# Moving the first load of a streaming row mean ahead of the program's opening barrier

## The chip, the cores and the metric

The kernel runs on one core of a Trainium2 chip (trn2). The metric is the device time of one execution in microseconds (us).

## The reference

```python
def setup_inputs():
    return {"x": np.random.randn(64, 256, 8192).astype(np.float32)}

def reference(x: np.ndarray) -> np.ndarray:
    return np.mean(x, axis=2)
```

The input is 64 x 256 x 8192 x 4 bytes = 536.87 MB, read once; the output is 64 KB. There is one addition per element read.

## The kernel before

The 16384 rows are cut into 64 blocks of 256 rows, two rows to each of 128 partitions (8.39 MB a block). SyncE issues all loads into three slots, VectorE sums each block with one reduce instruction, and ScalarE helps only near the end. The last block is loaded in shrinking pieces, so that little work is left when the last byte has landed.

```python
ROWS, SLOTS, LOAD_SEMS = 2, 3, 6
FETCH_BLOCK = 128
LAST_CHUNKS = (4096, 2048, 1024, 512, 256, 256)
# ...
    slots = [nc.alloc_sbuf_tensor(f"xt{i}", [P, R, S], F32) for i in range(SLOTS)]
    load_sem = [tc.alloc_semaphore(f"load{i}") for i in range(LOAD_SEMS)]
    # ...
    nc.vector.addr_align(FETCH_BLOCK, offset=0, max_nops=0)   # VectorE's stream is aligned
    # ... identity matrix on GpSimd, two small memsets on VectorE
    def load(dst, src, sem):
        ld = untracked(nc.sync.dma_start(out=dst, in_=src))
        # ... (kept out of the framework's own semaphores)
        ld.then_inc(sem, 16)
        return ld
    # ...
    for n in range(LB):                                       # LB = 63
        xt = slots[n % SLOTS]
        load(xt[:], x_v[n], load_sem[n % LOAD_SEMS])
        if n < LB - 1:
            loaded(n, dve_sum(res[:, :, n], xt[:]))           # waits for load n
        # ... last block, transposes and stores
```

The framework puts a head in front of this body: each engine loads its registers, GpSimd fills four small constant tiles (0.24 to 0.44 us in the trace of before), each engine executes a drain that reports to a barrier (the first at 0.00 us, the last, GpSimd's own, done at 0.49), and nobody enters the body before GpSimd has collected all reports and released them (at 0.61 us; the others go on at 0.66 to 0.67).

## Time and profile before

| What | Value | Where it is read |
|---|---|---|
| device time | 1248.35 us median of 3 (1248.23 to 1248.42) | times |
| span | 1246.8 us | page |
| bytes over span | 431 GB/s, 99.6% DMA share | page |
| VectorE busy | 87% | page |
| first load issued | 0.74 us | chain, timeline |
| first load bytes move | 1.77 us | trace of DMA packets |
| first sum starts | 23.15 us | timeline |

These lines are from the page of the kernel before: the span, busy tenths of VectorE and of the DMA engines in 40 slices, GB/s per slice, the chain of waits by engine, and the costliest group (busy us, mean ns of one, then idle us before it and what ended it).

```profile
span 1246.8 us, 224 instructions
...
DVE  2898988989889889898898988989889888898897
...
DMA  9999999999999999999999999999999999999998
GB/s 404 437 437 437 435 431 418 431 437 437 437 437 437 435 433 418 429 437 437 437 437 437 435 431 414 435 437 437 437 437 435 437 429 416 435 437 437 437 437 339
...
DMA 70%; DVE 29%; SPq 0%; issue 0%; DVEq 0%
...
L95 DVE TENSOR_REDUCE res<-xt 128x2 f32<-128x16384 f32 (+1 forms) x63 | 1076.4, 17086 | 154.0 <-DMA xt<-in_x_dram 154.0
```

The DMA line is full from the first slice to the last but one, 99.6% over the span. VectorE looks busy but waits for a load before every sum: 63 waits, 154.0 us in total. So the stream is the limit. It moves 431 GB/s over the span and 437 in 22 of the 40 slices, the most that any slice of this trace shows. Whether it can be made faster was not tested here; as long as it is not, what remains is the time before it starts and the time after it ends.

The head is easiest to see in the chain of waits (start us, length us, what). In these views DVE is VectorE; SPq, DVEq and PEq are the instruction queues of SyncE, VectorE and TensorE; "issue" is time in which an engine waited for nothing that the profile shows. This is the chain of the kernel before, its head and its end:

```profile
0.67 0.07 issue
0.74 22.39 DMA xt<-in_x_dram
23.12 0.02 issue
23.15 17.23 DVE res L95
...
1203.09 38.48 DMA xt<-in_x_dram
1241.58 0.02 issue
1241.60 0.69 DVE fin_in L95
...
1243.66 0.21 DVE fin_t L112
```

Nothing in the chain comes before 0.67 us: that is where the barrier releases SyncE. SyncE's own list of waits (engine and line, waited for: us in total, times, longest) names the wait (PEq, TensorE's queue, is the last engine to report to GpSimd, at 0.32 us; the trace has GpSimd let the engines go at 0.61 us), and the busy table by stretches (start:end and length in us, five engines, then clock, DMA share, GB/s) shows that no byte moves in the first 1.7 us:

```profile
SPq L176 <- PEq L176: 0.7, 1, 0.7
```

```profile
0.00:1.00 1.00, 0.00 (x0) 0.00 (x0) 0.00 (x0) 0.00 (x0) 0.41 (x5) 1.00 0.00 0
1.00:1.70 0.70, 0.00 (x0) 0.00 (x0) 0.13 (x2) 0.00 (x0) 0.29 (x1) 1.00 0.00 0
1.70:3.00 1.30, 0.00 (x0) 0.00 (x0) 0.00 (x0) 0.00 (x0) 0.00 (x0) 1.00 2.32 807
```

The GB/s of a short stretch is not a rate, because a packet of 65536 bytes is booked where it starts, and the first sixteen of this trace take 2.4 to 3.4 us (3.0 in the mean). Zero is zero, however.

### The profile page before, as it was taken

Reading aid. Unit: us, or ns where it says so; the run is one execution under the profiler, and the core shown is the slowest. Engines: PE = TensorE matmul, PEld = TensorE weight load, DVE = VectorE, ACT = ScalarE, POOL = GpSimd, SP = SyncE. Lnnn points to the kernel's source line nnn. Section 1 sums busy time; section 2 is a strip of 40 time slices with the busy share of each in tenths; the row PEclk is TensorE's granted clock in tenths of the full one; section 3 lists DMA queues with packets and bytes.
Section 4 is the critical chain, followed back from the end, with each engine's and each line's share of the span. In section 5 each row is a group of like instructions: output and inputs, shape, how many; then the busy total and the mean of one; then the engine's idle time right before and its main releaser. Section 6 shows DMA issues by size and latency. Waiting matters only on the chain.

```text
span 1246.8 us, 224 instructions
## 1 busy us (share of the span) xinstructions
PE 0.9 (0%) x2; PEld 0.4 (0%) x2; DVE 1087.3 (87%) x79; ACT 16.5 (1%) x13; POOL 0.7 (0%) x6
## 2 busy tenths in 40 slices
PE   0000000000000000000000000000000000000000
PEld 0000000000000000000000000000000000000000
DVE  2898988989889889898898988989889888898897
ACT  0000000000000000000000000000000000000004
POOL 0000000000000000000000000000000000000000
DMA  9999999999999999999999999999999999999998
GB/s 404 437 437 437 435 431 418 431 437 437 437 437 437 435 433 418 429 437 437 437 437 437 435 431 414 435 437 437 437 437 435 437 429 416 435 437 437 437 437 339
DMA packets 10169, 536.95 MB, mean 431 GB/s; under 512 B 1145, under 2 KB 1464, under 8 KB 1720
## 3 DMA queue, kind: packets, MB, share of 16 engines
q1 hardware_dynamic: 10168, 536.94, 99.6%
q14 instruction: 1, 0.01, 0.0%
HBM read 536.87 MB, written 0.07 MB: 431 GB/s over the span
## 4 chain that ended last, share of the span: by engine, by line
DMA 70%; DVE 29%; SPq 0%; issue 0%; DVEq 0%
DMA xt<-in_x_dram 70%; DVE res L95 29%; DVE fin_in L95 0%; SPq L85 0%; DVE fin_in L101 0%; DVE fin_t L112 0%; DVEq L101 0%
## 5 line engine op out<-in xcount | busy, mean ns | idle before, releaser
L95 DVE TENSOR_REDUCE res<-xt 128x2 f32<-128x16384 f32 (+1 forms) x63 | 1076.4, 17086 | 154.0 <-DMA xt<-in_x_dram 154.0
L98 ACT ACT_TABLE_LOAD x1 | 1.3, 1283 | 1182.5 <-DVE res L95 1182.5
L98 ACT ACTIVATE xt<-xt 128x8192 f32<-128x8192 f32 (+5 forms) x6 | 14.7, 2443 | 43.9 <-DMA xt<-in_x_dram 43.7
L95 DVE TENSOR_REDUCE fin_in<-xt 128x1 f32<-128x256 f32 (+3 forms) x5 | 4.9, 1003 | 0.3 <-DMA xt<-in_x_dram 0.2
L95 DVE TENSOR_REDUCE head<-xt 128x1 f32<-128x4096 f32 x1 | 4.4, 4420 | 0.2 <-DMA xt<-in_x_dram 0.2
L154 PE MATMUL ps<-ident,res 128*63 128x128 f32 x2 | 0.9, 458 | 1231.5 <-ACT xt L98 1230.4
L75 DVE MEMSET fin<- 128x32 f32 x2 | 0.1, 85 | 1.4 <-PEq L176 1.4
L98 ACT ACTIVATION_READ_ACCUMULATOR xt<-xt 128x1 f32 x6 | 1.1, 186 | 0.0
L155 DVE TENSOR_SCALAR bulk<-ps 63x128 f32<-63x128 f32 x2 | 0.6, 278 | 0.4 <-PE ps L154 0.4
L154 PEld LDWEIGHTS ps<-ident,res 128*63 128x63 f32 x2 | 0.4, 180 | 1231.8 <-issue 1230.4
L101 DVE TENSOR_SCALAR_CACHE_REDUCE fin_in<-fin_in 128x265 f32<-128x265 f32 x1 | 0.4, 431 | 0.2 <-DVE fin_in L95 0.2
L112 DVE STREAM_TRANSPOSE fin_t<-fin 128x32 f32<-128x32 f32 x2 | 0.4, 211 | 0.1
L63 POOL TENSOR_SCALAR_AFFINE_SELECT ident<-ident 128x128 f32<-128x128 f32 x1 | 0.3, 292 | 0.1
L101 DVE TENSOR_SCALAR_CACHE_REDUCE head<-head 128x2 f32<-128x2 f32 x1 | 0.2, 155 | 0.1
L62 POOL MEMSET ident<- 128x128 f32 x1 | 0.2, 204 | 0.3 <-POOLq L176 0.3
L176 POOL MEMSET const-bfloat16-1.0<- 128x1 bf16 x1 | 0.1, 101 | 0.0
L176 POOL MEMSET const-uint8-127<- 128x1 uint8 x1 | 0.1, 101 | 0.0
L176 POOL MEMSET const-float32-0.0<- 128x1 f32 x1 | 0.1, 98 | 0.2 <-issue 0.2
L176 POOL MEMSET const-float32-1.0<- 128x1 f32 x1 | 0.1, 98 | 0.0
L101 DVE DVE_READ_ACCUMULATOR head<-head 128x1 f32 x1 | 0.1, 83 | 0.0
L101 DVE DVE_READ_ACCUMULATOR fin_in<-fin_in 128x1 f32 x1 | 0.1, 83 | 0.0
## 6 DMA issues: line engine op xcount, KB each, us to landing
xt<-in_x_dram SPq DMA_DIRECT2D x1, 4096.0 KB, 31.1
xt<-in_x_dram SPq DMA_DIRECT2D x1, 2048.0 KB, 35.7
xt<-in_x_dram SPq DMA_DIRECT2D x1, 1024.0 KB, 37.7
xt<-in_x_dram SPq DMA_DIRECT2D x63, 40.8
xt<-in_x_dram SPq DMA_DIRECT2D x1, 512.0 KB, 38.5
xt<-in_x_dram SPq DMA_DIRECT2D x1, 256.0 KB, 38.7
xt<-in_x_dram SPq DMA_DIRECT2D x1, 128.0 KB, 38.5
fin_in<-in_x_dram SPq DMA_DIRECT2D x1, 128.0 KB, 38.4
```

The lines of the kernel that those rows point to most:

```text
L62: nc.gpsimd.memset(ident[:], 0.0)
L63: nc.gpsimd.affine_select(out=ident[:], in_=ident[:], compare_op=mybir.AluOpType.not_equal, fill=1.0, base=0, pattern=[[-1, P]], channel_m ...
L75: nc.vector.memset(fin[r][:], 0.0)
L95: return untracked(nc.vector.tensor_reduce(out=dst, in_=src, axis=X, op=ADD))
L98: return untracked(nc.scalar.activation(out=src, in_=src, func=COPY, accum_out=dst))
L101: return nc.vector.tensor_scalar(out=src, in0=src, scalar1=inv, scalar2=None, op0=mybir.AluOpType.mult, op1=ADD, accum_out=dst,)
L112: nc.vector.transpose(out=fin_t[r][:], in_=fin[r][:])
L154: nc.tensor.transpose(out=ps[:LB, :], in_=res[:, r, :], identity=ident[:])
L155: nc.vector.tensor_scalar_mul(out=bulk[:LB, :, r], in0=ps[:LB, :], scalar1=inv)
L176: nc = _bacc.Bacc("TRN2", target_bir_lowering=False, num_devices=1)
```

## The change

The first load needs nothing that the barrier guards: its slot has not been touched and its semaphore is its own. The change takes this one instruction out of the body and puts it into the head, in front of SyncE's barrier drain. No instruction is added or removed.

```diff
     for n in range(LB):
         xt = slots[n % SLOTS]
-        load(xt[:], x_v[n], load_sem[n % LOAD_SEMS])
+        ld = load(xt[:], x_v[n], load_sem[n % LOAD_SEMS])
+        if n == 0:
+            first = ld
# ... at the end of the kernel:
+    ctx.close()
+    tc.close()
+    tc.compile()
+    head_bb, body_bb = nc.main_func.blocks[:2]
+    assert first.ins in body_bb.instructions
+    body_bb.instructions.remove(first.ins)
+    at = next(
+        i
+        for i, ins in enumerate(head_bb.instructions)
+        if ins.engine == first.ins.engine and isinstance(ins, mybir.InstDrain)
+    )
+    head_bb.instructions.insert(at, first.ins)
```

## The prediction

> **What bounds the kernel.** The stream from HBM. The page reports 431 GB/s over the span, a DMA share of 99.6%, and 9 or more tenths in all 40 slices but the last. VectorE is busy 87%, but in the list of waits its sums wait for loads 63 times, 154.0 us in total. In the chain of waits, loads take 70% and sums 29%; the sums are there because a load needs a free one of three slots. Each sum ends about 2.1 us before the next load lands. A load takes 40.8 us from issue to landing, about two load pitches of 19.35, so it queues behind others and the queue never runs dry. Where the stream starts sets where it ends; the last landing in the chain (1241.58 us) leads into a tail of 5.2 us to 1246.8.
>
> **The head, before.** SyncE's barrier record comes first (time 0); the other engines reach the barrier at 0.12 to 0.32 us, GpSimd's drain ends at 0.49, and SyncE is released at 0.66 (SyncE's list of waits: 0.7 us). The first load is issued at 0.74, its issue takes 0.42, and the first packet moves at 1.77, 1.03 us after the issue began. Loads two and three are issued at 1.23 and 1.67.
>
> **What the change does.** By the order of instructions only SyncE's stream differs: the first load stands before the barrier's drain. Nothing is added or removed. The load needs nothing that the barrier guards: its slot is untouched and its semaphore its own.
>
> - Off the critical path: the 0.74 us between SyncE's first record and the first load. I expect the issue at 0 to 0.05 us, first packets at 1.0 to 1.1, and every later landing 0.7 earlier.
> - Moved onto the barrier: one issue slot, 0.49 us (738 to 1226 ns). SyncE then arrives at about 0.5 us, about when GpSimd's drain ends, so the release slips by at most 0.1 us. This is off the critical path: the second load is issued before 0.9 us, while the first takes some 21 us to move.
> - The drain now stands behind a load: [...] I expect no wait for the landing. No run shows this yet.
>
> **Predicted time.** Stream and tail shift as one: 1248.35 - 0.70 = 1247.65 us, 0.06% faster; several times the spread of the three runs (0.2 us), far inside 2%. Range 1247.2 to 1248.3. Chances: faster by over 2% 0.002, within 2% 0.994, slower by over 2% 0.004.
>
> **What would show it.** First load issued near 0, first packets near 1.05; the first sum at about 22.4 instead of 23.15; the release near 0.7; all sums ahead of before by a constant 0.7; an unchanged tail of 5.2 us; span near 1246.1; GB/s barely changed.
>
> **What would make it wrong.** (1) The drain waits for the landing: the barrier is released near 22 us, the second load is late, the stream idles about 2 us, and the time is near 1250. (2) The issue ahead of the barrier costs more than 0.42 us, or its packets come later than 1.03 us after it. (3) Launch, not SyncE's first record, starts what is timed: if SyncE's first instruction comes later, the gain shrinks. (4) Another phase of the stream changes its rate: slices differ between 414 and 437 GB/s, and 0.1% of rate outweighs the gain.

The 2 us of idling under (1) is an estimate; the run with the forced wait below measured 2.0.

## The result and the profile after

| | before | changed |
|---|---|---|
| device time, median (range, runs) | 1248.43 us (1248.23 to 1248.86, 6) | 1247.71 us (1247.58 to 1247.82, 6) |
| span of the profiled run | 1246.8 us | 1246.0 us |
| first load issued | 0.74 us | 0.00 us |
| first load bytes move | 1.77 us | 1.04 us |
| barrier releases SyncE | 0.655 us | 0.740 us |
| second load issued | 1.23 us | 0.83 us |
| first sum starts | 23.15 us | 22.46 us |

The ratio is 0.9994 with a 95% interval of 0.9981 to 1.0007. (A ratio is the mean time of one kernel's runs over that of the other's of the same rounds, so it is not quite the ratio of the medians quoted.) The interval includes 1, yet the slowest changed run, 1247.82 us, lies below the fastest run of before, 1248.23, and the same holds in the repetition below.

The page of the changed kernel: the stream looks as before, only the span is 0.8 us shorter.

```profile
span 1246.0 us, 224 instructions
...
DMA  9999999999999999999999999999999999999998
GB/s 434 425 421 438 438 438 436 438 427 417 438 438 438 438 438 436 429 414 438 438 438 438 438 436 431 412 438 438 438 438 438 436 431 417 433 438 438 438 438 339
...
DMA 70%; DVE 29%; SPq 0%; issue 0%; DVEq 0%
```

The chain of the changed kernel now begins with the load itself, at 0.00, and every later piece stands earlier:

```profile
0.00 22.43 DMA xt<-in_x_dram
22.43 0.02 issue
22.46 17.23 DVE res L95
...
1202.25 38.48 DMA xt<-in_x_dram
1240.73 0.02 issue
1240.76 1.45 DVE fin_in L95 x3
...
1242.82 0.21 DVE fin_t L112
```

The load takes the same time from issue to landing (22.43 against 22.39 us), and from the last landing of the chain to the end of the span it is 5.2 us in both kernels (1246.81 - 1241.58 before, 1245.97 - 1240.73 after). SyncE's wait at the barrier and the stretches of the head, in the changed kernel:

```profile
SPq L193 <- PEq L193: 0.2, 1, 0.2
```

```profile
0.00:1.00 1.00, 0.00 (x0) 0.00 (x0) 0.00 (x0) 0.00 (x0) 0.39 (x5) 1.00 0.00 0
1.00:1.70 0.70, 0.00 (x0) 0.00 (x0) 0.12 (x2) 0.00 (x0) 0.31 (x2) 1.00 3.47 1217
```

SyncE now spends 0.49 us of the old wait on issuing the load, and the first packets fall into the second stretch.

### The profile page after: what moved, and what is told of

Read it like the earlier page. It is cut to its first block, busy times and chain, and to the rows that moved or that the text cites. A ratio compares the mean times of both kernels' runs of the same rounds, so it can differ in the third digit from the quotient of the medians.

```text
span 1246.0 us, 224 instructions
## 1 busy us (share of the span) xinstructions
PE 0.9 (0%) x2; PEld 0.4 (0%) x2; DVE 1087.3 (87%) x79; ACT 16.4 (1%) x13; POOL 0.7 (0%) x6
## 4 chain that ended last, share of the span: by engine, by line
DMA 70%; DVE 29%; SPq 0%; issue 0%; DVEq 0%
DMA xt<-in_x_dram 70%; DVE res L95 29%; DVE fin_in L95 0%; SPq L85 0%; DVE fin_in L101 0%; DVE fin_t L112 0%; DVEq L101 0%
```

## The experiments

The theory is that the time follows the moment at which the first packet moves, one for one, and that nothing else in the change matters. Rivals: the gain comes from the load's place ahead of the barrier rather than from its moment; a later barrier release costs something of its own; a late start is partly absorbed; or the gain is luck of the runs. Each run below has five timed executions and gave the correct result; "difference" is the mean of its runs minus the mean of the 9 runs of before on the same chip. The spread of single runs is about 0.5 us, so such a difference has a standard error of roughly 0.1.

### Both kernels again

Edit: none. Kernel before against itself:

> The kernel before against itself: the floor of the comparison. Theory and rivals alike: a difference of under 0.2 us. Its trace also tells whether the lead of the changed kernel, 0.69 us at the first sum and 0.85 from the sixth on, is partly the scatter of one trace of before: then this trace differs from the first trace of before by 0.1 to 0.2 us at those sums; if it agrees within 0.03 us, the change itself won the extra 0.16.

Measured: median 1248.59 us, difference +0.14. That is the floor. Its trace differs from the first trace of before by +0.14 us at the second sum and by -0.18 from the seventh on. So the step in the lead of the changed kernel (0.69 us at the first sums, 0.85 from about the seventh on) is within what two traces of one kernel differ by, and I do not explain it.

The changed kernel:

> The changed kernel once more, unaltered, as the mark for the other runs of this call. Theory (the time follows the moment at which the first load is issued): 0.70 to 0.85 us below before, 1247.6 to 1247.8. Rival (no true gain, the first comparison was luck of the runs): within 0.2 us of before, and the two kernels' runs overlap.

Measured: median 1247.74 (1247.51 to 1248.01) against 1248.59 (1248.33 to 1248.94), difference -0.82, and again no overlap. The gain is real; two measurements give 0.75 and 0.82.

### The moment or the place: a delayed load ahead of the barrier

```diff
+        if n == 0:
+            hold = [untracked(nc.sync.drain()) for _ in range(16)]
         ld = load(xt[:], x_v[n], load_sem[n % LOAD_SEMS])
# ... and in the head, in front of the moved load:
+    for h in hold:
+        body_bb.instructions.remove(h.ins)
+        head_bb.instructions.insert(at, h.ins)
```

> The first load stands ahead of the barrier as in the change, but sixteen drains without a wait on SyncE stand ahead of it and hold it for a time d, which the trace will show (my guess is 0.5 to 1.0 us). Theory: the moment counts, so the time is that of the changed kernel plus d, about that of before if d is near 0.74, although the barrier is released later still. Rival A (the place ahead of the barrier is what pays, for instance because the barrier then overlaps with the load): 1247.7 as the changed kernel. Rival B (the later release of the barrier costs time too): more than d above the changed kernel.

Measured: the drains follow each other every 52 ns, so the load was issued at 0.84 us and the barrier released at 1.58. The time was 1248.04 us, difference -0.49: neither the changed kernel's (-0.82) nor before's (0). The first sum started at 23.24 us, within 0.1 of before, as the theory has it, and the last small sum at 1242.56 us, between the two traces of before (1242.63 and 1242.40). But the span from there to its end was 3.70 us instead of 4.18. The place gave nothing; an unexpected 0.5 us was won at the other end.

### The cost that the change takes away, doubled and more

```diff
         if n == 0:
+            for _ in range(HOLD):              # 16, then 64; kernel before, behind the barrier
+                untracked(nc.sync.drain())
```

> The kernel before with the same sixteen drains after the barrier, ahead of the first load: the cost that the change takes away, doubled or so. Theory: before plus d, one for one, near 1249.2 if d is near 0.74, with every landing late by the same d up to the end. Rival (the stream or the slack of VectorE absorbs a late start): less than half of d, below 1248.8.

> As the run with sixteen drains after the barrier, with sixty-four: d four times as long (a guess is 2 to 4 us). Theory: before plus d with a slope of 1, near 1251. Rival (absorbed, at least in part): a slope well below 1. Third possibility: fetching sixty-four more instructions delays SyncE beyond the drains themselves, which would be seen as a gap between drains in the trace.

Measured: issue at 1.57 us (0.83 later than before) and difference +0.04; issue at 4.05 us (3.31 later) and difference +2.32. Taken at face value this is the rival, "partly absorbed", and the one-for-one expectation missed twice, by 0.8 and 1.0 us. The traces show two things that came with the drains. First, the same shortened tail, 3.69 us in both. Second, the first load itself was quicker. These are its lines in the chain with 16 and with 64 drains:

```profile
1.57 22.04 DMA xt<-in_x_dram
```

```profile
4.05 22.02 DMA xt<-in_x_dram
```

In before it is 22.39 and in its repetition 22.51. So 0.49 us at the tail and about 0.4 us at the first load have to be explained before these runs can be read. (The profiled run with 16 drains is the slowest of its five, 1249.06 us, and its sums lose about 0.6 us between 62 and 140 us; I read only its head and tail.)

### The tail: sixteen drains where SyncE waits anyway

```diff
+        if n == SLOTS - 1:                     # changed kernel, after the third load
+            for _ in range(16):
+                untracked(nc.sync.drain())
```

> The changed kernel with sixteen drains on SyncE after the third load, where SyncE waits 38 us anyway. The three runs with drains ahead of the first load were all faster than their first packet's delay allows: from the start of the last small sum to the end of the span they took 3.70 us, all other kernels 4.18 to 4.23. Theory T (sixteen instructions more on SyncE, wherever they stand, move its stream so that the gap of 0.44 us between two of its drains at the end, and the long second drain, disappear): the tail is 3.7 us and the time near 1247.25, 0.4 to 0.5 below the changed kernel. Rival (the drains ahead of the load changed something else): tail 4.2 us and 1247.7.

Measured: median 1247.09 us (1246.98 to 1247.32) against 1248.41 of before, ratio 0.9989, difference -1.39. It is the lowest time and beats both kernels; every one of its runs is below the fastest of the changed kernel, 1247.51. Its chain ends as that of the changed kernel, at the same moment, but the span is shorter. The header of the chain and the chain's last piece, changed kernel:

```profile
core 0 of [0], span 1246.0 us
...
1242.82 0.21 DVE fin_t L112
```

and with sixteen drains after the third load:

```profile
core 0 of [0], span 1245.5 us
...
1242.81 0.21 DVE fin_t L113
```

What lies between is SyncE's closing sequence. In the changed kernel SyncE's drain at 1244.68 is followed by the next one only at 1245.11, and that one lasts 0.11 us; in the kernels with more instructions on SyncE the next drain follows after 0.06 us and lasts 0.01. At the same time one instruction-fetch packet of 8192 bytes changes its place: without the drains it goes out near the end of the span (1245.87 us in the changed kernel), with 16 more instructions on SyncE at 1148 to 1150 us, with 64 at 223 us. The 48 instructions between the last two moved that fetch by 927 us, which is 47.9 load pitches of 19.35 us, and SyncE issues one load per pitch.

Counting SyncE's records gives the same place in all fourteen traces: the fetch goes out after the 79th record and, where SyncE waits for a sum there, before the 80th. Without added drains the gap, of 0.43 to 0.45 us, stands between these two records as well; in the two runs below that add a single instruction it comes one instruction earlier, before the first drain and not after it. Gap and fetch are therefore tied to SyncE's place in its own stream, and without the drains that place falls into the closing sequence. The run shows that moving it away from there takes 0.49 us off. What SyncE does in the gap no record says. It does not wait for the bytes of that packet: in the changed kernel the packet goes out 0.75 us after SyncE has gone on.

### The first load: an instruction fetch among its packets

Every trace has another fetch packet of 8192 bytes after the barrier's release. In before it goes out at 4.88 us, in the changed kernel at 6.62, in the two runs with drains behind the barrier at 1.92 us, ahead of the load's first packet. A load raises its semaphore sixteen times, and the trace has each time:

| Load and run | fetch packet goes out | 15th landing after the first | 16th landing |
|---|---|---|---|
| first load, before | 4.88 us, during it | 0.45 us | 0.98 us |
| first load, changed | 6.62 us, during it | 0.60 us | 1.04 us |
| first load, 16 drains | 1.92 us, ahead of it | 0.46 us | 0.74 us |
| first load, 64 drains | 1.92 us, ahead of it | 0.57 us | 0.65 us |

The guess was VectorE's fetch, because VectorE's stream jumps over its alignment padding just after the barrier (its branch is recorded 0.11 us after SyncE's release, at 0.76 us in before and 0.85 in the changed kernel). To move it:

```diff
# changed kernel; VectorE's alignment goes ahead of VectorE's barrier drain
+    align = next(i for i in body_bb.instructions if type(i).__name__ == "InstAddrAlign")
+    body_bb.instructions.remove(align)
+    # at = place of VectorE's drain in the head
+    head_bb.instructions.insert(at, align)
```

> The changed kernel with VectorE's alignment (a jump over padding) moved from behind the barrier to ahead of VectorE's barrier drain. In all traces one instruction-fetch packet of 8192 bytes goes out about 1.27 us after the barrier's release; where loads are moving it waits behind a 64 KB packet, takes 0.31 us, and from that load on the last of the sixteen landings trails the fifteenth by 0.4 to 0.7 us; where the load that lands has seen no fetch the trail is 0.06. Theory F (this fetch, VectorE's, delays the stream by about 0.4): the fetch goes out ahead of the first packet at 1.04 us or near it, the trail at the first load falls below 0.3, and the time is 1247.2 to 1247.5. Rival 1 (the fetch belongs to another engine or comes just as late): packet after 1.1 us, trail and time as the changed kernel. Rival 2 (the trailing engine is slow for another cause): fetch early, trail still 0.4 or more, 1247.7.

> Both of the last two edits. If both theories hold and the two gains add: 1246.8 to 1247.0, about 1.6 us below before, the best of this study. If only the tail holds: 1247.25. If neither: 1247.7.

(The "about 1.27 us after the barrier's release" of the first text holds in the runs with drains behind the barrier, where no load is moving yet: 0.65 to 1.92. In before and in the changed kernel the packet goes out 4.2 and 5.9 us after the release, each time within 0.01 us of the end of a load packet's record: at 4.881 us, where a load packet ends at 4.884, and at 6.616, where one ends at 6.620. It takes 0.31 us in both. This is all that these two traces show of the waiting.)

Measured: 1247.81 (difference -0.78) and 1247.30 us (difference -1.20). The fetch went out at 4.21 us in the first of them, one load packet earlier than in the changed kernel (2.41 us, where a packet in mid-stream takes 2.42), but still behind the first load packet at 1.02, and the first load's sixteenth landing still trailed the fifteenth by 0.60 us. The edit moved the fetch, so the fetch goes with VectorE's jump; it did not move it far enough, and the time stayed. Whether an early fetch pays was not tested by these. One more run gives the fetch room: the same edit on the kernel with sixteen drains ahead of the moved load, whose first packet comes only at 1.88 us.

> The kernel with sixteen drains ahead of the first load, which stands ahead of the barrier, with one more edit: VectorE's alignment is moved ahead of its barrier drain. Without that edit this kernel took 1248.04 us; its fetch packet went out at 7.4 us, between load packets. With the alignment early, VectorE's fetch should be asked for at 1.1 to 1.3 us, while the first load packet comes only at 1.88. Theory F (a fetch that lands among the load packets costs the stream about 0.4 us): the packet goes out before 1.88 us, the sixteenth landing of the first load trails the fifteenth by less than 0.3 us instead of 0.45, the stretch from the first packet to the first sum is 21.0 us instead of 21.36, and the time is 1247.6 to 1247.7. Rival (the trail has another cause, and the two runs with drains behind the barrier were short for other reasons): packet early, but trail, stretch and time as without the edit, 1248.0 to 1248.1. If the packet still comes after 1.88 us, the question stays open.

Measured: the fetch went out at 1.26 us. The first load's line in the chain without that edit, and with it:

```profile
0.84 22.38 DMA xt<-in_x_dram
```

```profile
0.84 22.01 DMA xt<-in_x_dram
```

The load was 0.37 us quicker, and the sixteenth landing trailed by 0.12 us. So the fetch among the load's packets did delay it here, by 0.37 us, and the sums below show that the delay stayed with the stream. All the traces agree: in the nine with a fetch among its packets the first load takes 22.38 to 22.60 us from issue to landing, in the five without 21.82 to 22.04. Two of the five are the late-barrier runs below: their fetch goes out at 26 us, and there the second load has the trail (0.61 us) and the first has none (0.06). But the time was 1247.86 us, a difference of -0.58 where the kernel without the edit had -0.49: a gain of 0.09 (0.26 in the traces' spans), not the 0.4 expected. The trace shows where part of the rest went. The lead over the kernel without the edit is 0.43 us at every sum from 100 us to 1146 us, and 0.26 us at every sum after SyncE's fetch at 1149 us: 0.17 us are given back at that fetch, in one step. My reading of the landings: without the edit the sixteenth landing trails the fifteenth by 0.26 us before that fetch and by 0.12 after it, so the fetch delayed a part of the load that was not the last; with the edit the trail grows from 0.15 to 0.27. In this pair of traces, then, the stream that already trailed lost 0.17 us less to SyncE's fetch; what is left between 0.26 and 0.09 is within the spread of the runs.

### Does the barrier matter?

Three loads in the head:

```diff
-        if n == 0:
-            first = ld
+        if n == 0:
+            first = []
+        if n < SLOTS:
+            first.append(ld)
# ... and all three are moved in front of SyncE's drain, in their order
```

> All three first loads ahead of the barrier; the barrier should be released about 1 us later than in the changed kernel. Theory (only the first packet's moment counts): 1247.7 as the changed kernel, within 0.15. Rival A (the later loads' issue matters as well): below 1247.5. Rival B (the release of the barrier is on the critical path): about 1248.6.

Measured: barrier released at 1.68 us, 0.94 later than in the changed kernel; median 1247.80 us, difference -0.66. Neither the earlier issue of the second and third load nor the later barrier shows.

The changed kernel with a wait for the first landing ahead of the drain, then the same with all three loads in the head:

```diff
         if n == 0:
             first = ld
+            landed = untracked(nc.sync.nop(nofuse=True))
+            landed._wait_ge(load_sem[0], 16)
# ... moved into the head, between the load (or the three loads) and SyncE's drain
```

> The changed kernel with a wait for the landing of the first load put ahead of SyncE's drain: what the prediction feared the drain itself would do. Theory (in the changed kernel the drain does not wait, and the barrier matters only if it starves the stream): barrier released near 22.5 us, first packet of the second load about 1 us later, a hole of 1 to 2 us in the stream, and 1 to 2 us over the changed kernel, near 1249.2. Rival (the barrier was never in the way of the stream): 1247.7.

> All three first loads ahead of the barrier and then the same wait for the first landing: the barrier is released near 22.5 us but the stream has two more loads queued. Theory: no hole in the stream, the first sum starts about 1 us late and catches up in the 2.1 us that VectorE idles before each sum, so 1247.7, within 0.2 of the changed kernel, although the barrier is 22 us late. Rival (a late barrier costs time of its own): above 1248.6.

Measured: with one load 1250.64 us, difference +2.08; with three 1247.80 us, difference -0.74. In both SyncE's wait for the landing ends at 21.8 to 21.9 us and the barrier is released at 22.1. The same stretch of the two runs, with DMA share and GB/s last, first one load ahead and then three (packets are booked where they start, so those that started before 20.40 and ran into the stretch do not count here):

```profile
20.40:23.10 2.70, 0.00 (x0) 0.00 (x0) 0.33 (x3) 0.00 (x0) 0.50 (x2) 1.00 0.07 24
```

```profile
20.40:23.10 2.70, 0.00 (x0) 0.00 (x0) 0.28 (x3) 0.00 (x0) 0.50 (x2) 1.00 0.90 388
```

And the second sum of each (start us, length us, in brackets the wait before it), again first one load ahead and then three:

```profile
44.49 17.22 DVE L95 TENSOR_REDUCE res<-xt 128x2 f32<-128x16384 f32 x1 [4.47 <-DMA xt<-in_x_dram]
```

```profile
41.85 17.22 DVE L95 TENSOR_REDUCE res<-xt 128x2 f32<-128x16384 f32 x1 [1.77 <-DMA xt<-in_x_dram]
```

A barrier that was 21 us late cost nothing here while loads were queued (-0.74 against -0.82 of the changed kernel), and 2.9 us when it starved the stream (+2.08 against -0.82); at the second sum the two traces differ by 2.6 us. I had expected 1 to 2 us. The packet records show what was missed. The first load's last packets end at 20.95 to 21.47 us, 21.22 in the mean of the last sixteen, and its last landing follows 0.35 us later. The second load is issued at 22.14, and its first sixteen packets start at 23.10 to 23.44, 23.24 in the mean: 2.0 us without packets. Then the restart costs again: these sixteen take 3.13 us each, where the same packets of the run with three loads ahead, in a stream that did not stop, take 2.42. That is 0.7 us more, and 2.0 + 0.7 = 2.7 us is my estimate of the cost. (At the start of the stream too the first sixteen are slower, 2.9 to 3.3 us in the mean of each trace.) The landing itself is only a part of the 2.0 us: from the end of the last packet's record to the last landing of the first load it is 0.34 to 0.48 us in all fourteen traces.

### All runs against one sum

With four terms read from the traces every run can be added up, as a difference from before: the issue of the first load against 0.74 us; -0.49 where SyncE's tail gap is gone; -0.4 where VectorE's fetch goes out ahead of the first packet; and the 2.7 of the starved stream.

| Run | issue | tail | early fetch | starved | sum | measured |
|---|---|---|---|---|---|---|
| changed kernel (two measurements) | -0.74 | | | | -0.74 | -0.75, -0.82 |
| load held by 16 drains, ahead of the barrier | +0.10 | -0.49 | | | -0.39 | -0.49 |
| 16 drains behind the barrier | +0.83 | -0.49 | -0.4 | | -0.06 | +0.04 |
| 64 drains behind the barrier | +3.31 | -0.49 | -0.4 | | +2.42 | +2.32 |
| three loads ahead | -0.74 | | | | -0.74 | -0.66 |
| three loads ahead, barrier after landing | -0.74 | | | | -0.74 | -0.74 |
| one load ahead, barrier after landing | -0.74 | | | +2.7 | +1.96 | +2.08 |
| 16 drains after the third load | -0.74 | -0.49 | | | -1.23 | -1.39 |
| alignment early | -0.74 | | | | -0.74 | -0.78 |
| alignment early, 16 drains after the third load | -0.74 | -0.49 | | | -1.23 | -1.20 |
| load held ahead of the barrier, alignment early | +0.10 | -0.49 | -0.4 | | -0.79 | -0.58 |

Ten of the eleven agree within 0.16 us, about the spread of the comparison (the kernel before against itself gave +0.14). The last is off by 0.21; SyncE's own mid-stream fetch accounts for 0.17 of it. The terms for tail and early fetch were taken from some of these very traces, so the table shows that they are consistent, not that they are independent. No run delays the first load without adding instructions, so the one-for-one slope rests on this sum.

## Why the prediction was right

- *The stream is the limit, so its start sets its end.* Right: a start 0.73 us earlier at the first packet (1.77 to 1.04) gave 0.72 to 0.85 us in the medians. The held load, issued at 0.84, put the first sum back within 0.1 us of before although it still stood ahead of the barrier.
- *Issue at 0 to 0.05 us, first packets at 1.0 to 1.1.* Right: 0.00 and 1.04. Of the 1.04 us, 0.42 is the record of the issue, and the first packet follows 0.62 us after its end.
- *The barrier slips by at most 0.1 us and this is off the critical path.* Right: 0.085 us, and the runs with the barrier at 1.68 and 22.1 us, each with three loads ahead of it, took 1247.80 us each where the changed kernel took 1247.74: with loads queued its lateness cost nothing that shows.
- *SyncE's drain does not wait for the landing.* Right: its record is 0.11 us long and the barrier is released at 0.74, not near 22. The load's own record had ended at 0.42, ahead of its first packet at 1.04. It is not quite free: without a load in front of it the same drain takes 0.007 us.
- *All sums ahead by a constant 0.7 us.* Not quite: 0.69 at the first four, 0.85 later. Two traces of the kernel before differ by as much, so nothing is to be read from it.
- *Unchanged tail, span near 1246.1 us, time 1247.65.* Right: 5.2 us, 1246.0 and 1247.71. That the time agrees to 0.06 us is in part luck: the difference itself is known to about 0.1.
- *If the drain waited, near 1250 us.* The forced version took 1250.64 us. The stream idled for 2.0 us, as forecast; the slower packets at the restart, 0.7 us, were not in the forecast.

What the prediction did not see are two costs of about the same size as the whole gain, in the same profile: an instruction fetch among the first load's packets (0.4 us) and SyncE's gap at the end (0.49 us).

## What to carry to other kernels

In a kernel like this one, which streams from the first to the last microsecond, look first at the moment of the first packet and at the work after the last landing; issue the first load before anything that it does not need, barrier included. Here that put the first packet 0.73 us earlier and took 0.72 to 0.85 us off the time. A barrier released at 22.1 us was harmless here while loads were queued and cost more than the idle time once they ran out: 2.0 us without packets, and about 0.7 us more because the first packets after the stop took 3.13 us instead of 2.42. When a delay is added to measure a slope, check head and tail of the trace as well: the instructions added here also moved instruction fetches, worth 0.49 us at the tail and about 0.4 us at the first load, where the effect under study was 0.75 to 0.82 us.
